# Weighted expert sums on TensorE: gate-diagonal matmuls into PSUM, LayerNorm statistics read from PSUM, and half-size loads

## The chip, the cores and the metric

The kernel runs on one core of one Trainium2 chip. Its engines are TensorE (PE, with its weight loads PEld), VectorE (DVE), ScalarE (ACT), GpSimd (POOL) and SyncE (SP), which here issues most DMA transfers. The metric is the device time of one execution in microseconds, as the median of three runs.

## The reference, cut to what matters

Two decoder layers; each ends in a mixture of experts whose two expert outputs per token are added, weighted by their gates, to the scaled residual, and normalized:

```
for layer in range(DEPTH):                      # 2 layers, 1024 tokens x 1024
    mix = gated_deltanet(...) or differential_attention(...)
    h = layer_norm(ALPHA * h + mix, ln_mix_g[layer], ln_mix_b[layer])
    ffn = hierarchical_moe(h, ...)              # y = sum over a token's 2 experts of gate * y_rows
    h = layer_norm(ALPHA * h + ffn, ln_ffn_g[layer], ln_ffn_b[layer])
```

All of it is float32. The change touches the last two lines, for both layers.

## The kernel before

Tokens stand in eight tiles of 128 rows (`NT = 8`). `experts` writes the expert outputs, unweighted, to a DRAM tensor, two rows per token (`y1` in the first layer, called layer 0 here, `y2` in layer 1). `combine` (L1785) then makes the sums and the normalization tile by tile. Its inner function `load` brings both expert rows of a tile (`yin`, 128 x 2 x 1024, 1 MB); the residual tile `c.h[t]` (a buffer named `mraw` in the profile) is already there for t < 5. `first` weights the first expert row on ACT (L1812) and makes two DVE steps out of the rest (L1815, L1816). `second` calls `normalize`, where DVE takes the statistics (L245, L247) and ACT computes 1/sigma in `rstd` (L232 to L237: a logarithm, an exponential and four small steps); what follows depends on `way`: 1 is DVE (L258), ACT (L260), POOL (L261); 2 is ACT and two POOL steps; 0 is two DVE steps (L258, L263). In layer 0 `second` also turns the tile with eight TensorE transposes into `hT`, the operand of the next projections, which the attention phase then uses; layer 1 writes the result.

An ACT function needs its table set to be active. The compiler puts a table load (ACT_TABLE_LOAD) ahead of an instruction whose function the active set lacks; for a logarithm or an exponential it may pick a set that lacks the other of the two. The kernel can also ask for a set by name. `first` does so at t == 0 (L1814): `natural_log_exp_and_others`, which holds both. Between that load in layer 0 and the next one no other set is asked for, so the attention phase, which comes next, runs with it: the softmax exponentials (L1114), and `norm`, which is called 32 times (8 heads, every second of 8 query tiles) and holds a square (L1140), a logarithm (L1143) and an exponential (L1144) on ACT, and a DVE step (L1145).

In the attention phase TensorE's instructions are interleaved: transposes of a softmax tile (`atr`, L1131), scores (L1100 to L1102), value products, and as filling the projections of the next heads (`pj`, L223 to L225), whose results ACT and DVE cast into two parts (`khh`/`kll`, `vT`). Each engine works its instructions off in the order that the scheduler has fixed; `tc.keep_in_program_order` and priorities bear on that order, and an instruction with no operands may move far in it.

Of the kernel before, what the change touches and what calls it, by code (L numbers as in the profile page):

```python
# [9 lines left out]
F32 = mybir.dt.float32  # L10
# [4 lines left out]
AF = mybir.ActivationFunctionType  # L15
OP = mybir.AluOpType
AX = mybir.AxisListType
PSUM = bass.MemoryType.PSUM

P = 128  # L20
D = 1024
T = 1024
KT = 8
NT = 8
# [3 lines left out]
ALPHA = 4.0 ** 0.25  # L28
# [23 lines left out]
CAH = 1  # L52

HA = ((2, 5), (2, 5))
YB = (3, 8)
LGT = 1
WAYS = ((1,) * 6 + (0,) * 2, (1,) * 6 + (0,) * 2, (1,) * 6 + (0,) * 2, (1, 2, 1, 2, 1, 2, 0, 0))
WB = 2
CAPS = (
    (96, 96, 80, 128, 128, 112, 112, 104, 96, 96, 88, 88, 80, 80, 80, 80) + (64,) * 8 + (56,) * 3 + (48,) * 5,  # L60
# [70 lines left out]
def instruction(i):  # L131
    return getattr(i, "ins", i)


def row_bc(ap, n):
    return bass.AP(tensor=ap.tensor, offset=ap.offset, ap=[[0, P], [1, n]])
# [91 lines left out]
def rstd(c, sd, mv):  # L228

    act = c.nc.scalar.activation  # L230
    r, v, w = (sd[:, i:i + 1] for i in range(3))
    act(w, mv[:, 1:2], AF.Ln, bias=c.ln_eps, scale=1.0)  # L232
    act(v, mv[:, 1:2], AF.Identity, bias=c.half_eps, scale=-0.5)
    act(r, w, AF.Exp, scale=-0.5)
    act(w, r, AF.Square)
    act(w, w, AF.Identity, bias=c.three_half, scale=v)  # L236
    act(r, r, AF.Copy, scale=w)  # L237


def normalize(c, lp, a, lg, lb, way):  # L240

    nc = c.nc
    st = lp.tile([P, 2, 6], F32, name="ln_st")
    for k in range(2):
        nc.vector.bn_stats(st[:, k, :], a[:, k * 512:(k + 1) * 512])  # L245
    mv = lp.tile([P, 2], F32, name="ln_mv")
    nc.vector.bn_aggr(mv, st)  # L247
    sd = lp.tile([P, 4], F32, name="ln_sd")
    rstd(c, sd, mv)
    r, m = sd[:, 0:1], sd[:, 3:4]  # L250
    if way == 2:
        nc.scalar.activation(m, mv[:, 0:1], AF.Copy, scale=-1.0)
        nc.scalar.activation(m, m, AF.Copy, scale=r)
        nc.scalar.activation(a, a, AF.Identity, scale=r, bias=m)
        nc.gpsimd.tensor_tensor(a, a, lg, OP.mult)
        nc.gpsimd.tensor_tensor(a, a, lb, OP.add)
        return
    nc.vector.scalar_tensor_tensor(a, a, mv[:, 0:1], lg, op0=OP.subtract, op1=OP.mult)  # L258
    if way == 1:
        nc.scalar.activation(a, a, AF.Copy, scale=r)  # L260
        nc.gpsimd.tensor_tensor(a, a, lb, OP.add)  # L261
    else:
        nc.vector.scalar_tensor_tensor(a, a, r, lb, op0=OP.mult, op1=OP.add)  # L263
# [573 lines left out]
def out_proj(c, res, part, layer, h_dram):  # L837
# [4 lines left out]
    with ExitStack() as es:  # L842
# [41 lines left out]
        def norm(n, t, a):  # L884
            normalize(c, lp, a, lg, lb, WAYS[layer][n])
            nc.sync.dma_start(h_dram[t * P:(t + 1) * P], a)
# [898 lines left out]
def combine(c, layer, h_dram, y_dram, dst, hT=None):  # L1785

    nc, tc, ins = c.nc, c.tc, c.ins
    with ExitStack() as es:
        yp = es.enter_context(tc.tile_pool(reuse_waits="tile", name="c_y", bufs=YB[layer]))
        lp = es.enter_context(tc.tile_pool(reuse_waits="tile", name="c_l", bufs=3))  # L1790
        ps = es.enter_context(tc.tile_pool(reuse_waits="tile", name="c_ps", bufs=2, space=PSUM))
        lg, lb = c.w.tile(), c.w.tile()
        c.h += [c.w.spare() for t in range(HA[layer][1], NT)]
        yv = y_dram.rearrange("(t p k) f -> t p k f", p=P, k=2)

        ys = []

        def load(t):

            ys.append(yp.tile([P, 2, D], F32, name="yin"))  # L1800
            with tc.issue_after(c.load0) if t else ExitStack():
                c.load0 = instruction(nc.sync.dma_start(ys[t], yv[t]))
                if t == LGT:
                    nc.sync.dma_start(lg, row_bc(ins["ln_ffn_g"][layer], D))
                    nc.sync.dma_start(lb, row_bc(ins["ln_ffn_b"][layer], D))
                if t >= HA[layer][1]:
                    nc.sync.dma_start(c.h[t], h_dram[t * P:(t + 1) * P])

        def first(t):
            n = TILES[layer].index(t)  # L1810
            y, a = ys[t], c.h[t]
            nc.scalar.activation(y[:, 0], y[:, 0], AF.Copy, scale=c.gates[:, n, 0:1])  # L1812
            if t == 0:
                tc.keep_in_program_order(nc.scalar.preload_act_table_set("natural_log_exp_and_others"))  # L1814
            nc.vector.scalar_tensor_tensor(a, a, ALPHA, y[:, 0], op0=OP.mult, op1=OP.add)  # L1815
            nc.vector.scalar_tensor_tensor(a, y[:, 1], c.gates[:, n, 1:2], a, op0=OP.mult, op1=OP.add)  # L1816
            return t, a

        def second(t, a):
            normalize(c, lp, a, lg, lb, WAYS[2 + layer][t])  # L1820
            store = nc.gpsimd if layer == 0 and WAYS[2][t] else nc.sync
            store.dma_start(dst[t * P:(t + 1) * P], a)
            if hT is not None:
                for gr in range(2):
                    pt = ps.tile([P, 4, P], F32, name="ctr")
                    for i in range(4):
                        k = gr * 4 + i
                        nc.tensor.transpose(pt[:, i], a[:, k * P:(k + 1) * P], c.ident)
                    sl = slice(t * P, (t + 1) * P)
                    kk = slice(gr * 4, gr * 4 + 4)  # L1830
                    nc.scalar.copy(hT[0][:, kk, sl], pt)
                    nc.vector.tensor_tensor(hT[1][:, kk, sl], pt, hT[0][:, kk, sl].bitcast(F32), OP.subtract)


        for t in range(NT):
            while len(ys) < min(NT, t + YB[layer]):
                load(len(ys))
            second(*first(t))
            if layer == 0 and t >= WB:
                c.bp.start(t - WB)  # L1840
    c.raw2.close()
# [25 lines left out]
def build(c, out):  # L1867
    nc, tc = c.nc, c.tc
    with ExitStack() as es:
# [11 lines left out]
        with ExitStack() as ws:  # L1881
            phase_a(c, ws, p1, h1)
            with ExitStack() as ms:
                experts_open(c, ms)
                routing(c, 0)
                c.first_b = [c.ins["w_kvq"][i] for i in (0, 16, 8)]
                experts(c, 0, h1, y1)
            bs = es.enter_context(ExitStack())
            hp = bs.enter_context(tc.tile_pool(reuse_waits="tile", name="hT", bufs=1))
            hT = [hp.tile([P, KT, T], F32R, tag=f"hT{i}", name=f"hT{i}") for i in range(2)]  # L1890
            ps = bs.enter_context(ExitStack())
            phase_b_open(c, ps)
            combine(c, 0, h1, y1, h2, hT)
        phase_b_attention(c, hT, hp, h2, p2)
        ps.close()
        with ExitStack() as ws:
            weights_open(c, 1, ws)
            out_proj(c, h2, p2, 1, h3)
            bs.close()
            with ExitStack() as ms:  # L1900
                experts_open(c, ms)
                routing(c, 1)
                experts(c, 1, h3, y2)
            combine(c, 1, h3, y2, out)
# [18 lines left out]
```

## Time and profile before

| what | value |
|---|---|
| time, median of 3 runs | 2758.09 us (2755.68 to 2760.45) |
| the profiled execution | 2756.32 us, span 2754.4 us |
| busy, of the span | PE 88%, DVE 55%, ACT 44%, POOL 20% |
| combine of layer 0 | about 1361 to 1434 us |
| attention phase | about 1434 to 1970 us |
| combine of layer 1, up to the end | about 2692 to 2754 us |

The span is the profiled part of the execution; 1.9 us lie around it. Shares over the whole span mix stages with different limits, so each of the three stages has to be read by itself.

### The profile page before, as it was taken

How to read it: one execution, taken by the hardware profiler on the slowest of the kernel's cores; microseconds unless marked ns; L12 is line 12 of the kernel's file. 1: busy time of each engine (PE TensorE's matmuls, PEld its weight loads, DVE VectorE, ACT ScalarE, POOL GpSimd, SP SyncE). 2: the span in 40 equal slices, each digit the busy share in tenths (PEclk: the TensorE clock that was granted, in tenths of full speed). 3: DMA queues.
4: the chain of work that ended last, by engine and by line, in shares of the span. 5: the costliest groups of instructions: out<-in, count | busy, mean ns of one | idle time of the engine just before them, and what ended most of it. 6: DMA issues, size and time to landing. Idle time of an engine off the chain costs nothing. (4 is left out here: it accounts for less than half of the span.)

```text
span 2754.4 us, 38782 instructions
## 1 busy us (share of the span) xinstructions
PE 2419.5 (88%) x13789; PEld 1647.4 (60%) x13789; DVE 1506.7 (55%) x2696; ACT 1213.4 (44%) x2173; POOL 550.5 (20%) x445
## 2 busy tenths in 40 slices
PE   8999999999979988889559999998987898999990
PEld 5777777776745544444248777776764464455560
DVE  4555555564547555555385676667436323333567
ACT  5455555543325544444255555555332212223454
POOL 3333333331212110110132111111011101111104
PEclk9999999999989999999769999999997999999995
DMA  4111111124779999999841111012536968899995
GB/s 146 49 58 51 55 59 47 58 76 130 252 257 351 392 386 381 384 380 397 339 157 45 31 33 39 32 32 82 165 145 245 399 232 341 304 352 361 361 362 226
DMA packets 195478, 564.00 MB, mean 205 GB/s; under 512 B 40400, under 2 KB 63184, under 8 KB 193232
## 3 DMA queue, kind: packets, MB, share of 16 engines
q1 hardware_dynamic: 178240, 515.07, 50.8%
q0 software_dynamic: 15168, 43.01, 4.5%
q10 hardware_dynamic: 1872, 3.40, 0.4%
q8 instruction: 110, 1.80, 0.3%
q14 instruction: 88, 0.72, 0.1%
HBM read 515.58 MB, written 52.89 MB: 206 GB/s over the span
## 5 line engine op out<-in xcount | busy, mean ns | idle before, releaser
L210 DVE TENSOR_TENSOR ml<-mraw,mh 128x1024 fp32r<-128x1024 f32 x300 | 357.1, 1221 | 248.0 <-ACT mh L210 228.2
L210 ACT CAST mh<-mraw 128x1024 fp32r<-128x1024 f32 x300 | 306.5, 1052 | 247.5 <-DMA mraw<-in_w 196.0
L210 PE MATMUL acc<-mh,xT 128*128 128x512 f32 (+5 forms) x976 | 328.5, 405 | 1.6 <-ACT mh L210 1.6
L210 PE MATMUL acc<-mraw,xTw 128*64 128x512 f32 x1184 | 288.8, 620 | 16.4 <-DVE xTw L210 16.3
L185 POOL TENSOR_TENSOR wl<-raw,wh 128x512 fp32r<-128x512 f32 x106 | 155.1, 1484 | 484.7 <-ACT wh L184 420.5
L210 PEld LDWEIGHTS acc<-mh,xT 128*128 128x128 f32 (+5 forms) x976 | 166.5, 171 | 87.9 <-issue 18.6
L223 PE MATMUL pj<-xh,wh 128*128 128x512 f32 x512 | 217.6, 425 | 0.0
L224 PE MATMUL pj<-xl,wh 128*128 128x512 f32 x512 | 209.2, 409 | 0.0
L225 PE MATMUL pj<-xh,wl 128*128 128x512 f32 x512 | 207.5, 405 | 0.1
L1581 POOL DMA_INDIRECT X<-h,xidx x69 | 71.5, 1037 | 679.2 <-PE mtw L210 354.5
L210 PE MATMUL acc<-ml,xT 128*128 128x512 f32 (+5 forms) x496 | 195.9, 399 | 0.8 <-DVE ml L210 0.8
L223 PE MATMUL pj<-hT,wh 128*128 128x512 f32 (+1 forms) x432 | 166.0, 384 | 8.9 <-DVE kll L1010 5.4
L224 PE MATMUL pj<-hT,wh 128*128 128x512 f32 (+1 forms) x432 | 167.9, 389 | 0.0
L210 PEld LDWEIGHTS acc<-mraw,xTw 128*64 128x64 f32 x1184 | 76.9, 139 | 151.7 <-issue 109.7
L225 PE MATMUL pj<-hT,wl 128*128 128x512 f32 (+1 forms) x432 | 162.4, 376 | 1.6 <-POOL wl L185 1.6
L210 PE MATMUL acc<-mh,hT 128*128 128x512 f32 (+5 forms) x480 | 159.1, 402 | 0.2
L210 PE MATMUL acc<-mraw,hTw 128*64 128x512 f32 x592 | 140.5, 618 | 14.1 <-ACT hTw L210 14.0
L408 DVE SCALAR_TENSOR_TENSOR cv<-pr,cw,cv 128x512 f32<-128x512 f32 x144 | 118.9, 826 | 50.7 <-ACT cv L405 48.7
L1114 ACT ACTIVATE e<-sc,sm 128x256 f32<-128x256 f32 (+7 forms) x128 | 94.5, 741 | 89.8 <-DVE sm L1112 89.4
L210 PEld LDWEIGHTS acc<-mh,hT 128*128 128x128 f32 (+5 forms) x480 | 82.6, 172 | 49.6 <-issue 14.6
L225 PEld LDWEIGHTS pj<-xh,wl 128*128 128x128 f32 x512 | 96.9, 189 | 19.9 <-POOL wl L185 0.6
L224 PEld LDWEIGHTS pj<-xl,wh 128*128 128x128 f32 x512 | 97.3, 190 | 17.9 <-issue 1.4
(407 smaller groups left out, 4923.9 us busy)
## 6 DMA issues: line engine op xcount, KB each, us to landing
mraw<-in_w SPq DMA_DIRECT2D x720, 512.0 KB, 10.7
raw<-in_w_in SPq DMA_DIRECT2D x32, 512.0 KB, 3.5
yin<-y SPq DMA_DIRECT2D x16, 1024.0 KB, 7.0
raw<-in_w_kvq SPq DMA_DIRECT2D x21, 512.0 KB, 3.5
h<-res SPq DMA_DIRECT2D x16, 512.0 KB, 3.2
p<-ores POOLq DMA_DIRECT2D x12, 512.0 KB, 4.3
res<-p SPq DMA_DIRECT2D x12, 512.0 KB, 5.5
mh<-in_w SPq DMA_DIRECT2D x12, 512.0 KB, 6.8
```

Source lines behind the costliest of these rows:

```text
L185: c.nc.gpsimd.tensor_tensor(l[:, s], src[:, s], h[:, s].bitcast(F32), OP.subtract)
L210: out = getattr(self.engine, name)(*args, **kwargs)
L223: mm(out, ah, bh, start=first, stop=False)
L224: mm(out, ah, bl, start=False, stop=False)
L225: mm(out, al, bh, start=False, stop=last)
L408: nc.vector.scalar_tensor_tensor(a, pr[:, 1 + j:513 + j], cw[:, idx, j:j + 1], a, op0=OP.mult, op1=OP.add)
L1114: nc.scalar.activation(e[:, 0:L], st[m][:, 0:L], AF.Exp, bias=sm[:, 2 + m:3 + m], scale=SC, accum_out=sm[:, 4 + m:5 + m])
L1581: c.last_gather = instruction(nc.gpsimd.indirect_dma_start(out=b.X[0:rows], out_offset=None, in_=h_dram, in_offset=bass.IndirectOffsetOnAx ...
```

## The change

`combine` makes the weighted sum on TensorE. Three DVE instructions build `diag`: 17 matrices of 128 x 128, sixteen with the gates of one tile and one expert slot on the diagonal, one with ALPHA. A tile's sum is then, for each half of 512 columns, a float32 matmul of `diag` with each of the two expert rows, and, where the new table `RESP` says 1, one with the residual (2 tiles in layer 0, 6 in layer 1; the other eight add the residual by one DVE step on PSUM). `SUMS` gives the number of PSUM buffers. `normalize` reads statistics and its first pass from that sum in PSUM. The expert rows are loaded in halves of 512 KB, `YB` counts halves, and layer 1 uses way 1 where it used way 2 in turn. The request for the table set stands ahead of the loops.

```diff
-YB = (3, 8)
+YB = (4, 16)
-WAYS = (..., (1, 2, 1, 2, 1, 2, 0, 0))
+WAYS = (..., (1,) * 6 + (0,) * 2)
+RESP = ((1, 1, 0, 0, 0, 0, 0, 0), (1, 1, 1, 1, 1, 0, 1, 0))
+SUMS = (2, 4)
...
-        nc.vector.bn_stats(st[:, k, :], a[:, k * 512:(k + 1) * 512])
+        nc.vector.bn_stats(st[:, k, :], src[:, k * 512:(k + 1) * 512])
...
-    nc.vector.scalar_tensor_tensor(a, a, mv[:, 0:1], lg, op0=OP.subtract, op1=OP.mult)
+    nc.vector.scalar_tensor_tensor(a, src, mv[:, 0:1], lg, op0=OP.subtract, op1=OP.mult)
...
+        diag = dp.tile([P, 2 * NT + 1, P], F32, name="diag")
+        nc.vector.tensor_scalar(diag[:, 2 * NT], c.ident, ALPHA, None, op0=OP.mult)
+        gates = c.gates.rearrange("p t k -> p (t k)")
+        for q in (slice(0, 4), slice(4, 2 * NT)):
+            n = q.stop - q.start
+            nc.vector.tensor_tensor(diag[:, q], c.ident[:, None, :].to_broadcast([P, n, P]),
+                                    gates[:, q, None].to_broadcast([P, n, P]), OP.mult)
...
-            ys.append(yp.tile([P, 2, D], F32, name="yin"))
+            ys.append([yp.tile([P, D], F32, name="yin") for k in range(2)])
...
-                c.load0 = instruction(nc.sync.dma_start(ys[t], yv[t]))
+                for k in range(2):
+                    c.load0 = instruction(nc.sync.dma_start(ys[t][k], yv[t][:, k]))
...
+        def add(t, w, src, start, stop):
+            for f in range(2):
+                h = slice(f * 512, (f + 1) * 512)
+                nc.tensor.matmul(sums[t][:, h], diag[:, w], src[:, h], start=start, stop=stop)
+
+        def residual(t):
+            if t < NT:
+                sums[t] = ps.tile([P, D], F32, name="sum")
+                if RESP[layer][t]:
+                    add(t, 2 * NT, c.h[t], True, False)
...
         def first(t):
             n = TILES[layer].index(t)
-            y, a = ys[t], c.h[t]
-            nc.scalar.activation(y[:, 0], y[:, 0], AF.Copy, scale=c.gates[:, n, 0:1])
-            if t == 0:
-                tc.keep_in_program_order(nc.scalar.preload_act_table_set("natural_log_exp_and_others"))
-            nc.vector.scalar_tensor_tensor(a, a, ALPHA, y[:, 0], op0=OP.mult, op1=OP.add)
-            nc.vector.scalar_tensor_tensor(a, y[:, 1], c.gates[:, n, 1:2], a, op0=OP.mult, op1=OP.add)
+            for k in range(2):
+                add(t, 2 * n + k, ys[t][k], k == 0 and not RESP[layer][t], k == 1)
+            if not RESP[layer][t]:
+                nc.vector.scalar_tensor_tensor(sums[t], c.h[t], ALPHA, sums[t], op0=OP.mult, op1=OP.add)
...
+        tc.keep_in_program_order(nc.scalar.preload_act_table_set("natural_log_exp_and_others"))
+        for t in range(SUMS[layer]):
+            residual(t)
         for t in range(NT):
-            while len(ys) < min(NT, t + YB[layer]):
+            while len(ys) < min(NT, t + YB[layer] // 2):
                 load(len(ys))
-            second(*first(t))
+            first(t)
+            second(t)
+            residual(t + SUMS[layer])
```

What the scheduler makes of it on ACT in the combine of layer 0, from the last instruction ahead of it (`lm`, of the attention's setup). Before:

```order
L981 ACT_TABLE_LOAD
L981 ACTIVATE lm<-lm 128x2
L1812 ACTIVATE yin<-yin,gates 128x1024
L1814 ACT_TABLE_LOAD
L1812 ACTIVATE yin<-yin,gates 128x1024
L232 ACTIVATE ln_sd<-ln_mv,ct_all 128x1
L233 ACTIVATE ln_sd<-ln_mv,ct_all 128x1
L234 ACTIVATE ln_sd<-ln_sd 128x1
L235 ACTIVATE ln_sd<-ln_sd 128x1
L236 ACTIVATE ln_sd<-ln_sd,ct_all 128x1
L237 ACTIVATE ln_sd<-ln_sd 128x1
```

And in the changed kernel (lines are three or four higher: L235 is the logarithm, L237 the exponential):

```order
L985 ACT_TABLE_LOAD
L985 ACTIVATE lm<-lm 128x2
L235 ACT_TABLE_LOAD
L235 ACTIVATE ln_sd<-ln_mv,ct_all 128x1
L236 ACTIVATE ln_sd<-ln_mv,ct_all 128x1
L237 ACT_TABLE_LOAD
L237 ACTIVATE ln_sd<-ln_sd 128x1
L238 ACTIVATE ln_sd<-ln_sd 128x1
L239 ACTIVATE ln_sd<-ln_sd,ct_all 128x1
L240 ACTIVATE ln_sd<-ln_sd 128x1
L264 ACTIVATE mraw<-mraw,ln_sd 128x1024
```

The request for the joint set (now L1860) has moved out of this place: it stands at the head of layer 0's `experts`, and again at the head of layer 1's, each time just ahead of the load that the experts' SiLU needs. From there on a logarithm and the exponential behind it each have a load of their own, in all sixteen tiles of the two combines.

ACT at one of the 32 calls of `norm` in the attention phase. Before:

```order
L1114 ACTIVATE e,sm<-sc,sm 128x896 x2
L1140 ACTIVATE sq<-po 128x256
L1143 ACTIVATE sq<-pr,ct_all 128x256
L1144 ACTIVATE sq<-sq 128x256
L1084 COPY vT<-pj 128x512
L1035 CAST vh<-vtr 128x512
```

In the changed kernel:

```order
L1118 ACTIVATE e,sm<-sc,sm 128x896 x2
L1144 ACTIVATE sq<-po 128x256
L1147 ACT_TABLE_LOAD
L1147 ACTIVATE sq<-pr,ct_all 128x256
L1148 ACT_TABLE_LOAD
L1148 ACTIVATE sq<-sq 128x256
L1088 COPY vT<-pj 128x512
L1039 CAST vh<-vtr 128x512
```

The order of the other instructions is the same; all 32 calls have these two loads (64 in all; one of them falls to the softmax exponential behind the logarithm). Over the whole program ACT's list holds 168 table loads where it held 72.

TensorE in the combine of layer 0. Before, `ctr` being the transposes and `pj` the first projection:

```order
L1758 UNCONDITIONAL_BRANCH
L1828 MATMUL ctr<-ct_all,mraw 128x128 x16
L223 MATMUL pj<-hT_12017,wh 128x256
L224 MATMUL pj<-hT_12018,wh 128x256
L225 MATMUL pj<-hT_12017,wl 128x256
```

In the changed kernel, `sum` being the new sums:

```order
L1828 MATMUL sum<-mraw,diag 128x512 x4
L1828 MATMUL sum<-yin,diag 128x512 x11
L1854 MATMUL ctr<-ct_all,mraw 128x128 x8
L1828 MATMUL sum<-yin,diag 128x512 x4
L1854 MATMUL ctr<-ct_all,mraw 128x128 x8
L1828 MATMUL sum<-yin,diag 128x512
L226 MATMUL pj<-hT_12017,wh 128x256
```

The last matmul of tile 2's sum now stands behind the transposes of tile 0, and that of tile 3 behind the transposes of tile 1; the sums of tiles 4 to 7 stand behind the first projection pieces, in the same manner.

## Rows read from the trace of the kernel before

**Rows 1.** By stage: length, then busy PE, PEld, DVE, ACT, POOL; clock; DMA.
```profile
1361.00:1434.00 73.00, 27.65 (x122) 23.81 (x123) 68.00 (x75) 41.91 (x92) 30.66 (x19) 0.55 0.62 231
1434.00:1970.00 536.00, 508.50 (x2783) 418.97 (x2782) 360.62 (x776) 295.93 (x658) 77.48 (x50) 0.99 0.14 44
2692.00:2754.40 62.40, 0.00 (x0) 0.00 (x0) 50.32 (x47) 29.29 (x69) 26.97 (x9) 0.50 0.61 244
```

**Rows 2.** What TensorE waited for, 1434 to 1970: total us, times, longest.
```profile
PE atr L1131 <- DVE e L1124: 16.3, 22, 1.5
```

**Rows 3.** Timeline of TensorE (start, us): a float32 matmul; a restart after idling.
```profile
231.90 1.02 PE L699 MATMUL pr<-sq,ct_all 128*128 128x512 f32 x2
232.76 0.38 PE L680 MATMUL sc<-qd,S 128*128 128x128 f32 x2
...
1429.86 0.58 PE L223 MATMUL pj<-hT,wh 128*128 128x256 f32 x1 [3.75 <-DVE kll L1010]
...
1434.93 0.31 PE L225 MATMUL pj<-hT,wl 128*128 128x256 f32 x1
```

**Rows 4.** Timeline of ACT around a table load in phase A.
```profile
161.66 0.28 ACT L685 ACTIVATE sq<-sc 128x128 f32<-128x128 f32 x1 [0.44 <-PE sc L681]
161.96 1.28 ACT L702 ACT_TABLE_LOAD   x1
163.25 0.63 ACT L702 ACTIVATE sq<-sq 128x512 f32<-128x512 f32 x1
```

**Rows 5.** Timeline of one head's four norms in the attention phase.
```profile
1600.69 0.47 ACT L1143 ACTIVATE sq<-pr,ct_all 128x256 f32<-128x256 f32 x1 [0.33 <-PE pr L1142]
...
1604.29 0.48 ACT L1134 CAST ah<-atr 128x384 fp32r<-128x384 f32 x1 [0.70 <-PE atr L1131]
...
1611.29 0.66 PE L1131 MATMUL atr<-ct_all,e 128*128 128x128 f32 x4 [0.46 <-DVE e L1124]
...
1616.84 0.47 ACT L1143 ACTIVATE sq<-pr,ct_all 128x256 f32<-128x256 f32 x1
...
1618.28 0.87 DVE L1124 SCALAR_TENSOR_TENSOR e<-e,sm 128x640 f32<-128x640 f32 x1
...
1619.31 0.73 PE L1131 MATMUL atr<-ct_all,e 128*128 128x128 f32 x5
...
1637.32 0.47 ACT L1143 ACTIVATE sq<-pr,ct_all 128x256 f32<-128x256 f32 x1 [0.79 <-PE pr L1142]
...
1638.49 0.59 ACT L1084 COPY vT<-pj 128x512 f32<-128x512 f32 x1 [0.24 <-PE pj L225]
...
1639.22 0.60 PE L1033 MATMUL vtr<-ct_all,vT 128*128 128x128 f32 x4
...
1655.73 0.47 ACT L1143 ACTIVATE sq<-pr,ct_all 128x256 f32<-128x256 f32 x1
...
1656.44 0.27 PE L1131 MATMUL atr<-ct_all,e 128*128 128x128 f32 x1
```

**Rows 6.** Timeline of POOL's last step and TensorE's transposes, layer 0.
```profile
1398.84 3.20 POOL L261 TENSOR_TENSOR mraw<-mraw 128x1024 f32<-128x1024 f32 x1 [2.41 <-ACT mraw L260]
...
1402.09 1.97 PE L1828 MATMUL ctr<-ct_all,mraw 128*128 128x128 f32 x8 [3.56 <-POOL mraw L261]
```

**Rows 7.** Timeline of the combine of layer 1, up to the last DVE instruction.
```profile
2693.05 0.80 SPq L1802 DMA_DIRECT2D yin<-y  x2
...
2704.15 0.29 ACT L232 ACTIVATE ln_sd<-ln_mv,ct_all 128x1 f32<-128x1 f32 x1 [2.63 <-DVE ln_mv L247]
...
2705.41 0.29 ACT L237 ACTIVATE ln_sd<-ln_sd 128x1 f32<-128x1 f32 x1
...
2706.61 1.15 ACT L260 ACTIVATE mraw<-mraw,ln_sd 128x1024 f32<-128x1024 f32 x1 [0.91 <-DVE mraw L258]
...
2712.62 1.29 DVE L245 BATCH_NORM_STATS2 ln_st<-mraw 128x6 f32<-128x512 f32 x2
...
2749.47 1.28 DVE L263 SCALAR_TENSOR_TENSOR mraw<-mraw,ln_sd 128x1024 f32<-128x1024 f32 x1 [0.31 <-ACT ln_sd L237]
```

More of the change, by code (lines that the diff above doesn't have):

```diff
@@ L54 @@
 HA = ((2, 5), (2, 5))
-YB = (3, 8)
+YB = (4, 16)
 LGT = 1
-WAYS = ((1,) * 6 + (0,) * 2, (1,) * 6 + (0,) * 2, (1,) * 6 + (0,) * 2, (1, 2, 1, 2, 1, 2, 0, 0))
+WAYS = ((1,) * 6 + (0,) * 2, (1,) * 6 + (0,) * 2, (1,) * 6 + (0,) * 2, (1,) * 6 + (0,) * 2)
+RESP = ((1, 1, 0, 0, 0, 0, 0, 0), (1, 1, 1, 1, 1, 0, 1, 0))
+SUMS = (2, 4)
 WB = 2
@@ L237, in rstd, with normalize @@
     act(r, r, AF.Copy, scale=w)
-def normalize(c, lp, a, lg, lb, way):
+def normalize(c, lp, a, lg, lb, way, src=None):
     nc = c.nc
+    src = a if src is None else src
     st = lp.tile([P, 2, 6], F32, name="ln_st")
     for k in range(2):
-        nc.vector.bn_stats(st[:, k, :], a[:, k * 512:(k + 1) * 512])
+        nc.vector.bn_stats(st[:, k, :], src[:, k * 512:(k + 1) * 512])
     mv = lp.tile([P, 2], F32, name="ln_mv")
@@ L253, in normalize @@
         nc.scalar.activation(m, m, AF.Copy, scale=r)
-        nc.scalar.activation(a, a, AF.Identity, scale=r, bias=m)
+        nc.scalar.activation(a, src, AF.Identity, scale=r, bias=m)
         nc.gpsimd.tensor_tensor(a, a, lg, OP.mult)
@@ L1790, in combine @@
         lp = es.enter_context(tc.tile_pool(reuse_waits="tile", name="c_l", bufs=3))
-        ps = es.enter_context(tc.tile_pool(reuse_waits="tile", name="c_ps", bufs=2, space=PSUM))
+        dp = es.enter_context(tc.tile_pool(reuse_waits="tile", name="c_d", bufs=1))
+        ps = es.enter_context(tc.tile_pool(reuse_waits="tile", name="c_ps", bufs=SUMS[layer], space=PSUM))
         lg, lb = c.w.tile(), c.w.tile()
+        diag = dp.tile([P, 2 * NT + 1, P], F32, name="diag")
[5 more added lines that the diff above has]
+                                    gates[:, q, None].to_broadcast([P, n, P]), OP.mult)
         c.h += [c.w.spare() for t in range(HA[layer][1], NT)]
@@ L1807, in load, with second @@
                     nc.sync.dma_start(c.h[t], h_dram[t * P:(t + 1) * P])
+        sums = {}
+        def add(t, w, src, start, stop):
[7 more added lines that the diff above has]
+                    add(t, 2 * NT, c.h[t], True, False)
         def first(t):
             n = TILES[layer].index(t)
-            y, a = ys[t], c.h[t]
-            nc.scalar.activation(y[:, 0], y[:, 0], AF.Copy, scale=c.gates[:, n, 0:1])
-            if t == 0:
-                tc.keep_in_program_order(nc.scalar.preload_act_table_set("natural_log_exp_and_others"))
-            nc.vector.scalar_tensor_tensor(a, a, ALPHA, y[:, 0], op0=OP.mult, op1=OP.add)
-            nc.vector.scalar_tensor_tensor(a, y[:, 1], c.gates[:, n, 1:2], a, op0=OP.mult, op1=OP.add)
-            return t, a
-        def second(t, a):
-            normalize(c, lp, a, lg, lb, WAYS[2 + layer][t])
+            for k in range(2):
+                add(t, 2 * n + k, ys[t][k], k == 0 and not RESP[layer][t], k == 1)
+            if not RESP[layer][t]:
+                nc.vector.scalar_tensor_tensor(sums[t], c.h[t], ALPHA, sums[t], op0=OP.mult, op1=OP.add)
+        def second(t):
+            a = c.h[t]
+            normalize(c, lp, a, lg, lb, WAYS[2 + layer][t], sums[t])
             store = nc.gpsimd if layer == 0 and WAYS[2][t] else nc.sync
@@ L1824, in second @@
                 for gr in range(2):
-                    pt = ps.tile([P, 4, P], F32, name="ctr")
+                    pt = c.bp.ps.tile([P, 4, P], F32, tag="tr", name="ctr")
                     for i in range(4):
```

## The prediction, made before the changed kernel was run

> **What bounds the kernel now.** I first read the table of stages. The combine of layer 0 (1361 to 1434) keeps DVE busy for 68.0 of 73 us, that of layer 1 (2692 to the end) for 50.3 of 62.4 with TensorE at rest, and the attention phase between them keeps TensorE busy for 508.5 of 536 us, ACT for 295.9 [rows 1]. So DVE sets the two combines and TensorE the attention phase. Next I read what TensorE waits for in that phase: mostly the softmax mix ahead of the transposes, 22 times and 16.3 us in all, 0.7 us each [rows 2]. That chain is tight: at 22 places there is no slack at all, and a delay of ACT or DVE goes through to TensorE.
>
> **What is removed.** One ACT pass for each of the sixteen tiles, and two DVE passes for each, of which eight tiles keep one on PSUM. DVE loses 24 passes of 1.28 us (the length of the last one in the trace [rows 7]), some 30 us over both stages, more where POOL slowed it. That is the gain if nothing else ends later.
>
> **What is added on TensorE.** A float32 matmul of 512 columns takes 232.76 - 231.90 = 0.86 us at full clock (2.4 GHz) [rows 3], twice that at the lower level (1.2 GHz). Layer 0 gets (8 x 2 + 2) x 2 = 36, layer 1 (8 x 2 + 6) x 2 = 44, that is 31 and 38 us at full clock. After a wait of 3.75 us TensorE ran at the lower level from 1429.86 to 1434.93, 5.1 us, before it rose [rows 3].
>
> **What is added on ACT, which only the program's list shows.** The request for the joint table set is hoisted to the head of `experts`, where the SiLU's load overwrites it. So there is a load for each logarithm and one for the exponential behind it: 16 in each combine, 64 in the attention phase. One in phase A takes 1.28 us; it starts 0.02 us after the instruction ahead has ended, and the exponential starts 0.01 us after it [rows 4]. So the price is 1.28 us each, with nothing around it. A load has no operand to wait for: the first of a pair can fill a gap that ACT has anyway; the second can't.
>
> The Trainium skill ("ScalarE: Activation LUTs", What ACT_TABLE_LOAD costs) gives the same 1283 ns but adds a drain of about 1380 ns, 2.66 us for each switch; by it the pairs would take about 170 us of ACT in the attention phase (an estimate from that page) where the row gives 82. Rows 4 show no such drain, and I go by them.
>
> **Attention, +54 us.** There are 32 norms; I follow the four of one head, which differ [rows 5].
> - At 1600.69 ACT had idled 0.33 us before the logarithm, so the exponential is 2.57 - 0.33 = 2.24 late, and the casts behind it too, until the cast of the transposes at 1604.29, before which ACT idled 0.70: 1.5 us are left. Score maxima, exponentials and the mix follow, and the transposes at 1611.29 wait already (0.46). Cost 1.5.
> - At 1616.84 ACT had no gap. DVE's step of the norm waits for the exponential, and the mix at 1618.28 stands behind it on DVE. It ended at 1619.15, the transposes began at 1619.31: 2.57 - 0.16 = 2.4.
> - At 1637.32 there is a gap of 0.79, and 0.24 before the copy at 1638.49, which the transposes at 1639.22 need: 1.5. TensorE works in order, so all behind them is late.
> - At 1655.73 there is no gap. The transposes at 1656.44 start 0.24 us after the logarithm ended; I take it that they need its PSUM buffer. One load stands before that: 1.3.
>
> Together 6.7 us a head, 54 for eight. The bounds: 19 if only the second kind reaches TensorE, 82 if all 64 loads do.
>
> **Layer 0's combine, +8 us.** DVE loses 10 passes (16 go, 6 come back), 12.8 us of its 68.0. ACT's 41.9 us lose eight passes of 1.15 [rows 7] and gain 16 loads: 53 of 73. Only two sums fit in PSUM, and the last matmul of tile t + 2 stands behind the transposes of tile t on TensorE, which wait for POOL, which waits for ACT. A round of two tiles is then: transposes 2.0 and POOL 3.2 [rows 6], the matmul, a DVE pass and statistics (2.8), `rstd` with its loads (4.1, below) and scale (1.15), about 15 us; the other tile's ACT work, 6.3 us with its two casts (0.48 for 384 columns [rows 5], more for 512), falls in between in part, so I take 17. Four rounds are 68; the first tile comes some 5 us later since TensorE starts cold, and the projection pieces ahead of the sums of tiles 4 and 6 add some 8 (48 matmuls of 256 columns at about 0.2 us, partly beside other work): 81 us in place of 73. Bounds: -8 (DVE still the limit, most of its 12.8 gone) and +20 (all 16 loads on the path).
>
> **Layer 1's combine, -2 us.** TensorE begins with 8 residual matmuls near 2693 [rows 7]: three in the cold 5.1 us, five at 0.86, then four for tile 0 by 2705.9, its statistics (1.29 [rows 7], 1.5 with the aggregation) by 2707.4; ACT began at 2704.15 before. From here DVE needs about 2.8 us a tile and TensorE 3.4 to 5.2, but ACT needs `rstd` 1.55 (2704.15 to 2705.41 + 0.29), two loads 2.57 and the scale 1.15 [rows 7]: 5.27 us for each of six tiles, 4.12 for the other two. ACT becomes the limit. Its first load is over before the statistics are: 2707.4 + 3.99 + 5 x 5.27 + 4.12 = 2741.9 for the seventh tile's `rstd`. Behind that stand, in DVE's order, its last pass (1.28), the last tile's statistics (1.5), its `rstd` (2.83, one load hidden) and last pass (1.28): 2748.8, against 2749.47 + 1.28 = 2750.8 [rows 7], which is -2.0. Bounds: -10 if TensorE is warm and ACT's loads are hidden in part; +14 if TensorE stays at the lower level (44 x 1.72 = 76 us from 2693, so its last sum at 2769, less what its waits for the rows would give back). The half-size loads bring the same bytes in the same order; only tile 0 could gain a fraction of a microsecond, which the cold TensorE hides. `diag` costs DVE three passes over 2176 columns in all, two microseconds or three, in layer 0 before the rows land, in layer 1 among the last experts.
>
> **Sum.** 54 + 8 - 2 = +60 on 2756.3, the profiled execution, 1.8 us under the median of the runs: 2816 on that scale, 2818 as a median. I say 2816.
>
> **Rivals.**
> - *The loads hide in attention* (faster). ACT has 240 us idle there and 82 are added [rows 1]. If the filling projections cover the delays, attention costs nothing and the combines decide: with DVE as their limit they give back 8 and 10 us, 2738. It decides where each norm's delay stays under the slack of the chain; rows 2 and the second norm of rows 5 show none. Chance 0.04; with a dearer combine, within 0.2% of 2758 (5.5 us, about what a measurement tells from no change), another 0.04.
> - *The loads do not come between logarithm and exponential.* ACT would need 2.7 us a tile in layer 1, and both combines would end early: 2738 too. Against it: phase A has such a load right ahead of an exponential [rows 4]. Chance 0.02. The Trainium skill ("ScalarE: Activation LUTs", Table sets: the hidden batching unit) says that a logarithm and the exponential behind it need one load, since one set has both; the trace disagrees here, as its rows show the second load.
> - *Each switch costs double.* A stall as long as the load, behind each one, would lift 54 to about 137 (64 x 1.3 more) and the combines by up to 30: 2900 to 2930. The gaps of rows 4 speak against it. Chance 0.03. The drain quoted above would do this.
> - *TensorE at its lower clock becomes the limit of both combines*: +14 and +20 on top of attention, 2844. For it: the granted clock was 0.55 and 0.50 in these stages [rows 1]. Against it: the new matmuls stand close together. Chance 0.12.
>
> **How the numbers follow.** The forecast with its bounds has 0.75. Attention is its widest term: between 25 and 75 us of it, with -3 to +14 for the combines, give 2778 to 2846, and that also holds half of the clock case, 8 in 10 together. Slower by over 0.2% has 0.90, no change 0.04, faster 0.06.
>
> **What would show it.** Table loads of 1.28 us at 64 places in attention; each head longer by some 6.7 us; TensorE waiting longer on the mix; in layer 1's combine ACT, not DVE, without gaps, and DVE near 2.8 us a tile. The forecast is wrong if the attention phase stays at 536 us, or if TensorE's clock in layer 1's combine stays at 0.50.

## The result, and the profile after

The changed kernel took 2804.15 us (median of four runs, 2802.54 to 2806.23) where the kernel before took 2758.11 beside it: a ratio of 1.017, 95% interval 1.0154 to 1.0186. The prediction said 2816, between 2778 and 2846. The profiled execution is the one of 2802.54 us, span 2800.4; against the span of before, 2754.4, that is +46.0.

The stages after, in the columns of [rows 1] (length; busy time of PE, PEld, DVE, ACT, POOL; clock; DMA). The attention phase now reaches to 2020:

```profile
1361.00:1434.00 73.00, 52.38 (x209) 31.20 (x208) 43.96 (x66) 53.67 (x100) 25.06 (x18) 0.90 0.66 241
1434.00:2020.00 586.00, 521.99 (x2765) 422.44 (x2765) 357.43 (x773) 376.56 (x719) 75.66 (x50) 0.98 0.13 41
2738.00:2800.40 62.40, 40.47 (x88) 17.57 (x88) 27.07 (x36) 39.96 (x70) 14.05 (x6) 0.83 0.62 244
```

DVE is down from 68.0 to 44.0 us in the combine of layer 0 and from 50.3 to 27.1 in that of layer 1, and TensorE runs there at a granted clock of 0.90 and 0.83 in place of 0.55 and 0.50. Yet neither stage is much shorter, since ACT has 12 and 11 us more; and the attention phase is 50 us longer. I measure the stages by marks that every kernel here has: a combine from the first load of expert rows on SP's queue to the last hT step on DVE (layer 0) or the end of the span (layer 1), the attention phase from the first norm's logarithm to the last one's.

| between the marks, us | before | after | |
|---|---|---|---|
| combine of layer 0 | 77.6 | 75.1 | -2.5 |
| attention, first to last norm | 492.7 | 543.4 | +50.7 |
| last norm to first load of layer 1's combine | 724.8 | 719.8 | -5.0 |
| combine of layer 1 | 61.4 | 62.0 | +0.6 |

Starts are read to a tenth of a us, so differences of these can be off by 0.1. The rest, +2.2, is a start of layer 0's combine that is 1.65 later and 0.6 between it and the first norm. What made the -5.0 is open: in the twelve kernels below that stretch took between 722 and 730 us, in one execution each, with or without the loads, a spread wider than the 5.0.

The groups of table loads on ACT by line, in the whole span (count; busy us, mean ns; idle time before them):

```profile
L1147 ACT ACT_TABLE_LOAD x32 | 41.1, 1283 | 0.6
L1148 ACT ACT_TABLE_LOAD x31 | 39.8, 1283 | 0.6
...
L235 ACT ACT_TABLE_LOAD x16 | 20.5, 1283 | 4.8 <-issue 4.5
L237 ACT ACT_TABLE_LOAD x16 | 20.5, 1283 | 0.3
...
L1118 ACT ACT_TABLE_LOAD x1 | 1.3, 1283 | 0.0
```

The 64 of the attention phase and the 32 of the combines are all there, each 1.283 us. What TensorE waited for from 1434 to 2030, against [rows 2] (total us, times, longest):

```profile
PE atr L1135 <- DVE e L1128: 32.9, 24, 2.4
PE vtr L1037 <- ACT vT L1088: 9.5, 8, 1.5
PE atr L1135 <- ACT sq L1147: 8.4, 9, 1.3
```

The wait on the mix has doubled (16.3 before). The two others are the third and the fourth norm of the prediction's head: the copy `vT` 1.2 us late on average, once for each head, a wait that TensorE did not have before; the logarithm 0.9 on average, nine times, where it was waited for once before (0.8 us).

The start of layer 1's combine on ACT, which answers to [rows 7]:

```profile
2738.57 1.28 ACT L235 ACT_TABLE_LOAD   x1 [4.51 <-issue]
2753.72 0.29 ACT L235 ACTIVATE ln_sd<-ln_mv,ct_all 128x1 f32<-128x1 f32 x1 [13.87 <-DVE ln_mv L251]
...
2754.22 1.28 ACT L237 ACT_TABLE_LOAD   x1
2755.52 0.20 ACT L237 ACTIVATE ln_sd<-ln_sd 128x1 f32<-128x1 f32 x1
...
2756.74 1.15 ACT L264 ACTIVATE mraw<-mraw,ln_sd 128x1024 f32<-128x1024 f32 x1
2757.90 1.28 ACT L235 ACT_TABLE_LOAD   x1
...
2763.37 1.28 ACT L235 ACT_TABLE_LOAD   x1
```

The first load is over long before the statistics, as predicted. From then on ACT has no gap for seven tiles and takes 5.47 us a tile (2757.90 to 2763.37), while DVE waits for it, 8.65 us in one place:

```profile
2752.15 1.30 DVE L249 BATCH_NORM_STATS2 ln_st<-sum 128x6 f32<-128x512 f32 x2 [17.36 <-PE sum L1828]
...
2789.56 1.28 DVE L267 SCALAR_TENSOR_TENSOR mraw<-mraw,ln_sd 128x1024 f32<-128x1024 f32 x1 [8.65 <-ACT ln_sd L240]
```

### The profile page after: what moved, and what is told of

Same layout as the page of the kernel before. It is cut to its first block, busy times and chain, and to the rows that moved or that the text cites. A ratio compares the mean times of both kernels' runs of the same rounds, so it can differ in the third digit from the quotient of the medians.

```text
span 2800.4 us, 39191 instructions
## 1 busy us (share of the span) xinstructions
PE 2502.9 (89%) x13949; PEld 1679.2 (60%) x13949; DVE 1462.0 (52%) x2681; ACT 1320.9 (47%) x2247; POOL 532.8 (19%) x442
## 4 chain that ended last, share of the span: by engine, by line
PE 46%; DMA 21%; DVE 14%; ACT 11%; issue 4%; POOL 2%; SPq 0%; ACTq 0%; another core or an unknown queue 0%; DVEq 0%; POOLq 0%
DMA mraw<-in_w 18%; PE acc L213 18%; PE pj L227 4%; PE pj L226 4%; PE pj L228 4%; PE po L227 2%; PE po L226 2%; PE po L228 2%; DVE tmp L558 2%; DVE cv L412 1%; ACT L1147 1%; DVE sm L1115 1%; PE atr L1135 1%; ACT e L1118 1%; DVE ml L213 1%
## 5 line engine op out<-in xcount | busy, mean ns | idle before, releaser
L213 PE MATMUL acc<-mraw,hTw 128*64 128x512 f32 x592 | 147.7, 644 | 22.8 <-ACT hTw L213 22.7
L412 DVE SCALAR_TENSOR_TENSOR cv<-pr,cw,cv 128x512 f32<-128x512 f32 x144 | 119.0, 827 | 50.9 <-ACT cv L409 48.9
L213 PEld LDWEIGHTS acc<-mraw,hTw 128*64 128x64 f32 x592 | 43.4, 147 | 112.3 <-issue 74.6
```

The costliest lines, as they stand in the source:

```text
L213: out = getattr(self.engine, name)(*args, **kwargs)
L412: nc.vector.scalar_tensor_tensor(a, pr[:, 1 + j:513 + j], cw[:, idx, j:j + 1], a, op0=OP.mult, op1=OP.add)
```

## The experiments

My theory: the loads, which came in because the request lost its place, cost all of the lengthening, and the sums on TensorE by themselves gain. The main rival: the sums, their clock, the PSUM operands or the smaller transfers cost something of their own. The first four kernels take the two apart.

**e1_pinned: the change with the request held in its place.**

```diff
         def first(t):
             n = TILES[layer].index(t)
+            if t == 0:
+                nc.scalar.copy(lp.tile([P, 1], F32, name="pin", bufs=1), ys[0][0][:, 0:1])
+                tc.keep_in_program_order(nc.scalar.preload_act_table_set("natural_log_exp_and_others"))
...
-        tc.keep_in_program_order(nc.scalar.preload_act_table_set("natural_log_exp_and_others"))
         for t in range(SUMS[layer]):
```

> The changed kernel with one thing put back: the request for the joint table set stands behind a one-column copy of the first expert row on ACT, so that it stays at the head of each combine and its set holds through the attention phase; ACT's list has 72 loads in place of 168. Theory (the loads are the cost): the attention phase gives back its 50.6 us, ACT needs about 2.9 us a tile in place of 5.5 in layer 1's combine, which ends about 8 us sooner, that of layer 0 some 5 us; the 4 us that the experts of layer 1 gained are lost again: 2804 - 51 - 8 - 5 + 4 = 2744 us, under the kernel before. Rival 1 (the loads are only beside the cost, which comes from the sums on TensorE, the statistics from PSUM or the half-size loads): 2804, unchanged. Rival 2 (the loads cost in the attention phase alone, the combines hide them): about 2757, level with the kernel before.

2739.4 us (2735.67 to 2742.06), ratio to before 0.993 (0.9917 to 0.9944): faster than before. Its norms, with the first and the last start, and its two combines:

```profile
L1147 ACT ACTIVATE sq<-pr,ct_all x32: 465/474/477, 1464.0 to 1958.4; 128x256 f32<-128x256 f32 x32
```

```profile
1358.00:1423.00 65.00, 52.25 (x211) 30.78 (x211) 46.11 (x73) 34.91 (x88) 25.13 (x18) 0.92 0.77 279
...
2683.60:2735.30 51.70, 40.38 (x88) 17.57 (x88) 26.96 (x36) 20.06 (x56) 14.11 (x6) 0.90 0.75 294
```

The theory had 2744. Attention is back at 494.4 us, and ACT has 20.1 us in place of 40.0 in layer 1's combine, which is 10.3 shorter; layer 0's is 11.0 shorter, where the theory had 8 and 5. One more line of the change, `pt = c.bp.ps.tile([P, 4, P], F32, tag="tr", name="ctr")`, is in every figure for the sums and is taken apart by no run: the transposes' result takes its PSUM buffers from the attention phase's pool and no longer from `combine`'s own, where the sums now are.

**e2_before_moved: the kernel before, with only the request moved.**

```diff
-            if t == 0:
-                tc.keep_in_program_order(nc.scalar.preload_act_table_set("natural_log_exp_and_others"))
...
+        tc.keep_in_program_order(nc.scalar.preload_act_table_set("natural_log_exp_and_others"))
         for t in range(NT):
```

> The kernel before with only the request moved ahead of the loops, as the change has it; sums, statistics and loads as before. Theory: the same 64 loads in the attention phase cost about 50 us there, the 16 in each combine up to 10 us each, since DVE, not ACT, sets those stages: 2806 to 2825, 2815 us. Rival (the loads cost nothing by themselves): 2758.

2823.65 us (2821.34 to 2827.34), ratio 1.0238 (1.022 to 1.0256). Its norms, with their loads:

```profile
L1143 ACT ACT_TABLE_LOAD  x32: 1283/1283/1283, 1483.1 to 2026.6; - x32
L1143 ACT ACTIVATE sq<-pr,ct_all x32: 474/474/477, 1484.4 to 2027.9; 128x256 f32<-128x256 f32 x32
```

Without any of the new sums the attention phase takes 543.5 us, as in the changed kernel. The combines lose 10.2 and 6.0 us; the theory had 2815 in all.

**e3_attn_pinned and e4_attn_loads: the loads in one half only.** The first holds the request at the head of the attention phase, the second (on e1_pinned) asks there for the exponential's own set:

```diff
-    nc.scalar.preload_act_table_set("natural_log_exp_and_others")
+    tc.keep_in_program_order(nc.scalar.preload_act_table_set("natural_log_exp_and_others"))
...
+    tc.keep_in_program_order(nc.scalar.preload_act_table_set("exp_and_others"))
```

> The changed kernel with the request at the head of the attention phase held in its place, behind the combine of layer 0: the 64 loads of the attention phase go, the 32 of the combines stay. Theory: 2804 - 51 + 4 = 2757 us, and the stage lengths of both combines as in the changed kernel (about 72 and 62 us). Rival (the attention phase became longer by what the combine leaves behind, not by its loads): 2804.

> The other half: the first of these kernels (request held in both combines) with a request for the exponential's own set at the head of the attention phase, so that the 64 loads come there and none in the combines. Theory: 50 us longer than the first of these kernels less the 4 us in layer 1's experts, about 2790 us, and its attention phase as long as in the changed kernel (543 us between the first and the last norm). Rival: as the first of these kernels.

2757.51 us (ratio 0.9998, 0.9986 to 1.0009) and 2789.96 us (1.0117, 1.01 to 1.0133). The six kernels side by side, in us between the marks:

| sums | loads | combine 0 | attention | combine 1 | median |
|---|---|---|---|---|---|
| DVE, ACT (before) | none | 77.6 | 492.7 | 61.4 | 2758 |
| DVE, ACT (e2) | both | 87.8 | 543.5 | 67.4 | 2824 |
| TensorE (e1) | none | 64.1 | 494.4 | 51.7 | 2739 |
| TensorE (e3) | combines | 75.2 | 493.8 | 62.3 | 2758 |
| TensorE (e4) | attention | 65.6 | 543.3 | 51.6 | 2790 |
| TensorE (after) | both | 75.1 | 543.4 | 62.0 | 2804 |

Each stage depends on its own loads alone. The sums give 13.5 and 9.7 us in the combines; the loads take 11 and 10.3 of that back, and cost 49 to 51 in attention. The main rival is out.

These are one profiled execution each, and a stage repeats itself only so well. In e1, e4 and the later e5, e9, e10 and e12 TensorE, DVE and POOL do the same instructions in the same order in layer 0's combine, without loads, and it took 64.1, 65.6, 63.2, 66.8, 65.1 and 67.8 us. So the sums give some 10 to 14 us there, and between two of these kernels a difference of under 4 us in that stage is not shown. Layer 1's combine is steadier: 51.4 to 52.2 us in e1, e4, e9, e10 and e12.

**e7_copied and e8_warm_before: where the 13.5 come from.** The first puts the sums back into SBUF ahead of the statistics, the second gives the kernel before matmuls whose result nobody reads:

```diff
+            nc.scalar.copy(a, sums[t])
-            normalize(c, lp, a, lg, lb, WAYS[2 + layer][t], sums[t])
+            normalize(c, lp, a, lg, lb, WAYS[2 + layer][t])
...
+            if layer == 0:
+                for f in (0, 512, 0, 512):
+                    nc.tensor.matmul(warm, c.ident, y[:, 1, f:f + 512], start=True, stop=True)
```

> On the kernel with the request held (2739 us): ACT copies each finished sum from PSUM into the tile in SBUF, and the statistics and the first pass read that copy, so that they are as before the change while the sums stay on TensorE. Adds 16 copies of about 1.15 us on ACT. Theory (reading PSUM is what freed DVE and POOL of each other: a pass took up to 3.4 us beside POOL before and 1.28 after, a POOL step 3.2 and 2.34): DVE passes from SBUF stretch to 2 us and more beside POOL again and POOL's steps to 3 us; combine of layer 0 about 70 in place of 64.2, layer 1 about 54 in place of 51.7: 2748. Rival (fewer passes alone freed them): passes stay at 1.28, only the copies' delay shows, 1 to 2 us a stage: 2742.

> The kernel before, with four float32 matmuls for each tile of layer 0's combine that read the expert row and write a PSUM tile which nobody reads; nothing else changes (DVE and ACT still make the sums). It asks what the higher granted clock gives by itself. Theory (DVE sets that stage, busy 68 of 73 us): transposes go from 1.97 to about 1.1 us, but the stage gets at most 2 to 3 us shorter than its 77.7: 2755 to 2758. Rival (the clock is most of the 13.5 us that the sums on TensorE gain there): 2747 to 2750. Rival (the matmuls delay the transposes): up to 2765.

e7_copied took 2744.29 us (ratio 0.9947, 0.9927 to 0.9966; e1_pinned 0.993). DVE's first pass and POOL's addition in layer 0's combine (count; busy us, mean ns; idle), of e1_pinned:

```profile
L262 DVE SCALAR_TENSOR_TENSOR mraw<-sum,ln_mv,mraw 128x1024 f32<-128x1024 f32 x8 | 10.2, 1279 | 1.4 <-DMA mraw<-in_ln_ffn_g 1.2
...
L265 POOL TENSOR_TENSOR mraw<-mraw 128x1024 f32<-128x1024 f32 x6 | 14.1, 2351 | 22.1 <-ACT mraw L264 22.1
```

and of e7_copied:

```profile
L262 DVE SCALAR_TENSOR_TENSOR mraw<-mraw,ln_mv 128x1024 f32<-128x1024 f32 x8 | 16.5, 2063 | 0.4
...
L265 POOL TENSOR_TENSOR mraw<-mraw 128x1024 f32<-128x1024 f32 x6 | 15.9, 2658 | 24.0 <-ACT mraw L264 23.9
```

The same pass takes 1.28 us with one operand in PSUM and 2.06 on average with both in SBUF (2.12 before the change). The averages hide two cases. Here is one pass beside one of POOL's additions in e7_copied, and then in e1_pinned:

```profile
1376.90 2.34 POOL L265 TENSOR_TENSOR mraw<-mraw 128x1024 f32<-128x1024 f32 x1 [16.04 <-ACT mraw L264]
1377.12 3.20 DVE L262 SCALAR_TENSOR_TENSOR mraw<-mraw,ln_mv 128x1024 f32<-128x1024 f32 x1
```

```profile
1372.10 2.36 POOL L265 TENSOR_TENSOR mraw<-mraw 128x1024 f32<-128x1024 f32 x1 [14.45 <-ACT mraw L264]
1372.24 1.28 DVE L262 SCALAR_TENSOR_TENSOR mraw<-sum,ln_mv,mraw 128x1024 f32<-128x1024 f32 x1
```

In e7_copied the two passes of that stage that met no work of POOL's took 1.28 us as well. The Trainium skill ("SBUF — State Buffer", SBUF: two separate sides) says that a DVE operation with two SBUF inputs and a GpSimd operation that reads SBUF exclude each other; the trace agrees, 3.20 against 1.28. So the theory holds for the passes. Its prices for the stages do not: layer 0's combine took 66.0 us where it had 70, which is within the scatter around e1_pinned, and layer 1's 57.4 where it had 54; the copies on ACT are in both, and the run doesn't tell what the passes cost by themselves.

e8_warm_before took 2755.18 us (ratio 0.9988, 0.9977 to 1.0). The granted clock of its combine is 0.80, that of before 0.54, and the stage is 74.4 us in place of 77.7, with DVE still at 66:

```profile
1358.00:1434.00 76.00, 52.67 (x197) 31.88 (x198) 66.42 (x79) 42.11 (x94) 30.02 (x19) 0.80 0.65 239
```

The clock, as far as it rose here, gives 3.3 us of the 13.5 by the stage and 2.1 by the time, both hardly more than the noise; the rival that had it as most of the gain (2747 to 2750) is out. I put what is left down to DVE's passes that are gone; no run takes these away by themselves.

**e6_whole_loads: transfers of 1 MB again.**

```diff
-                for k in range(2):
-                    c.load0 = instruction(nc.sync.dma_start(ys[t][k], yv[t][:, k]))
+                c.load0 = instruction(nc.sync.dma_start(y, yv[t]))
```

> On the kernel with the request held (2739 us): expert rows come by one transfer of 1 MB for each tile again, as before the change, in as many buffers. Theory (as predicted: same bytes in the same order): within 1 us in both combines, 2739 to 2740. Rival (halves let the first sum start earlier): combine of layer 0 longer by 2 to 3 us, that of layer 1, where the residual matmuls cover the landing, unchanged: 2742.

2737.86 us (ratio 0.9926, 0.9907 to 0.9945), not to be told from e1_pinned. Layer 0's combine took 67.2 us, from a first load that went out 3 us sooner to the same end, 1422.4. That is the 2 to 3 us more that the rival had and not the 1 of the theory; but it lies within the stage's scatter, and the instructions of the stage stand in another order too, so neither is shown there. Layer 1's took 51.5, as both had it.

**e9_first_only, e10_second_only, e12_both_planned: one load or the other.** Requests of their own in the norm of e1_pinned; the third kernel has both:

```diff
+            tc.keep_in_program_order(nc.scalar.preload_act_table_set("natural_log_exp_and_others"))
             nc.scalar.activation(sq, pr, AF.Ln, bias=c.rms_eps, scale=1.0 / P)
+            tc.keep_in_program_order(nc.scalar.preload_act_table_set("natural_log_exp_and_others"))
             nc.scalar.activation(sq, sq, AF.Exp, scale=-0.5)
```

> The kernel with the request held (2739 us, attention 494.4 us from the first norm's logarithm to the last) with one table load put in ahead of each of the 32 norms' logarithms, none between logarithm and exponential. By the gaps that the prediction counts, such a load costs 1.28 less 0.33 and 0.70 at the first norm of a head (0.25), 1.12 at the second, 0.25 at the third, 1.28 at the fourth: 2.9 us a head, 23 us for eight, 2762. Rival (each load costs alike, half of the 50.7 that both cost): 25, 2765. Rival (ACT's wait for the matmul of the squares hides it wholly): under 5, 2740 to 2744.

> The same with the 32 loads between logarithm and exponential, where ACT has no wait to fill. By the prediction's gaps: 0.58 at the first norm of a head (1.28 less 0.70), 1.12 at the second, 1.04 at the third (1.28 less 0.24), none at the fourth, where the transposes wait for the logarithm alone: 2.7 us a head, 22 us, 2761; with the 23 of the other half that is less than the 50.7 of both, since a gap filled by one load is not there for the second. Rival (each load costs alike): 25, 2765. Rival (only the second load costs): 45 to 50, 2785 to 2790.

2755.52 us (ratio 0.999, 0.9979 to 1.0001) and 2753.34 (0.9965, 0.9942 to 0.9987). Their norms:

```profile
L1148 ACT ACTIVATE sq<-pr,ct_all x32: 468/477/480, 1466.3 to 1974.9; 128x256 f32<-128x256 f32 x32
```

```profile
L1147 ACT ACTIVATE sq<-pr,ct_all x32: 468/477/478, 1465.9 to 1969.5; 128x256 f32<-128x256 f32 x32
```

Attention takes 508.6 and 503.6 us, +14.2 and +9.2, against the 23 and 22 that I worked out, and together far less than the 49 of e4_attn_loads. But these requests stand in the program when its order is set. By the traces TensorE, ACT and DVE go through the attention phase in another order than in e1_pinned, while in the changed kernel they keep that of e1_pinned, the loads apart. Hence the last run.

> The kernel with the request held (2739 us, attention 494.4 us between first and last norm) with both loads put in as requests of their own, one ahead of each logarithm and one ahead of each exponential: the same 64 loads at the same places as in the changed kernel. There the loads were put into a list whose order was set without them (TensorE's, DVE's and POOL's orders are those of the kernel with the request held, instruction for instruction); here, as with the two halves, the requests are there when the order is set, and projections and transposes change places around the norms. Theory 1 (the order, made with the loads in it, puts other work of TensorE where the norms are late): the halves add up, 14.2 + 9.2 = 23 us, attention 518 us, 2763. Theory 2 (a delay is free up to the slack of the chain, about a microsecond, and each one beyond it counts, whatever the order): as in the changed kernel, attention 543 us, 2788.

2768.32 us (ratio 1.0044, 1.0028 to 1.006), and attention 525.5:

```profile
L1148 ACT ACTIVATE sq<-pr,ct_all x32: 473/474/476, 1464.8 to 1990.3; 128x256 f32<-128x256 f32 x32
```

That is +31.1, between the two theories: 18 of the 49 us go when the order is made with the loads in it, and 31 remain, 8 more than the halves add up to. Two loads that share one slack would have it so; but the orders of the three kernels differ among themselves as well, so that is not shown.

**e5_res2 and e11_dve_only: from here to a faster kernel.** In e1_pinned TensorE has no gap in layer 1's combine, and its first 9.48 us go to residuals while DVE waits:

```profile
2684.27 9.48 PE L1828 MATMUL sum<-mraw,diag 128*128 128x512 f32 x16 [5.68 <-issue]
2693.58 7.03 PE L1828 MATMUL sum<-yin,diag 128*128 128x512 f32 x16
```

```diff
-RESP = ((1, 1, 0, 0, 0, 0, 0, 0), (1, 1, 1, 1, 1, 0, 1, 0))
+RESP = ((1, 1, 0, 0, 0, 0, 0, 0), (1, 1, 0, 0, 0, 0, 0, 0))
```

e11_dve_only also sets the third entry of `WAYS` to `(0,) * 8`. That gives DVE the last step of all eight tiles of layer 0; the entry chooses the queue of the stores too, so all eight tiles are stored from SP's queue where six had gone from POOL's.

> On the kernel with the request held (2739 us): in layer 1 only the first two tiles keep their residual on TensorE, the other six get it as a DVE pass on PSUM, as layer 0 has it. There TensorE had no gap from 2684.3 to 2724.6 while DVE waited 17 us for the first sum. Theory (TensorE is the limit of that combine now): 8 matmuls of 0.86 us go, 4 of them ahead of the first sum at the lower clock, and DVE, with 4.05 us for such a tile, ends about 5 us sooner: combine 51.7 to about 46, 2734 us. Rival (the rows from DRAM are the limit, their loads moving 294 GB/s over the stage): no change, 2739. Rival (DVE becomes the limit at once, four more passes of 1.23): up to +3, 2742.

> On the fastest kernel so far (request held, two residuals on TensorE in layer 1, 2732 us): in layer 0's combine DVE makes the last step of all eight tiles by itself (one pass of 1.28 us, as it does for the last two), in place of ACT's scale (1.15) and POOL's addition (2.35) for six. Theory (that stage is set by the way from statistics to transposes, TensorE waits 5 times for POOL and DVE is idle for a third of it): a tile's way is 2.2 us shorter, DVE has 50 of some 60 us, and the stage ends 4 to 6 us sooner: 2727. Rival (DVE becomes the limit there): 0 to +3, 2732 to 2735.

e5_res2: 2731.99 us (ratio 0.9902, 0.9885 to 0.9919), layer 1's combine 46.9. Its first two rows on TensorE:

```profile
2687.68 5.98 PE L1828 MATMUL sum<-mraw,diag 128*128 128x512 f32 x8 [5.59 <-issue]
2693.50 27.63 PE L1828 MATMUL sum<-yin,diag 128*128 128x512 f32 x64
```

e11_dve_only: 2730.47 us (0.9896, 0.9879 to 0.9913), not to be told from it. The theory had 4 to 6 us off layer 0's combine, and it was wrong: the stage took 66.2 us where that of e5_res2 took 63.2, with DVE at 52.7 of them and the clock at 0.86 in place of 0.93. The 3.0 are within the stage's scatter, so that it became longer is not shown, and neither is why nothing was gained.

## Why the prediction was right, by its steps

**Attention, +54: the loads are the cause, the size 50.7.** e2, e3 and e4 give 50.8, 49.6 and 48.9 for the same 64 loads. The first six heads took 7.0 us more each (their 24 norms 417.8 us for 375.5) where the prediction had 6.7. The second head before, and the second and third after, in the columns of [rows 1]:

```profile
1538.12:1600.69 62.57, 59.97 (x321) 49.01 (x320) 43.46 (x95) 35.90 (x81) 9.69 (x6) 1.00 0.11 34
```

```profile
1545.13:1614.93 69.80, 61.17 (x322) 48.70 (x321) 43.63 (x94) 46.09 (x89) 9.71 (x6) 1.00 0.10 31
1614.93:1684.35 69.42, 62.31 (x322) 50.15 (x321) 42.84 (x94) 46.28 (x89) 9.19 (x6) 0.98 0.10 31
```

What TensorE waited for in the second head, before and after:

```profile
PE atr L1131 <- DVE e L1124: 2.4, 3, 1.5
```

```profile
PE atr L1135 <- DVE e L1128: 5.6, 4, 2.4
PE vtr L1037 <- ACT vT L1088: 1.2, 1, 1.2
PE atr L1135 <- ACT sq L1147: 1.1, 1, 1.1
PE pj L226 <- DVE kll L1014: 0.5, 1, 0.5
```

So the waits are those that the prediction named, and each is somewhat shorter: 3.2 us more on the mix for its 1.5 and 2.4, 1.2 for the copy's 1.5, 1.1 for the logarithm's 1.3, together 5.5 for 6.7. A wait on `kll` (0.5) that it did not name, and 1.2 us more of busy time on TensorE, for which no run here shows a reason, bring the head to 7.2. That the total fits so well is in part luck. In four of the first six heads the mean granted clock was 0.98 and in two 1.00; the four took 69.4 to 69.9 us and the two 69.8, so the clock is not what lengthened them.

The prediction was too high for the last two heads: from 1851.01 to 1968.21 before and 1892.99 to 2018.56 after, they cost 8.4 together and not 13.4; why they are cheaper I did not test. That the gaps in single rows also give the price of one load alone is not borne out (14.2 and 9.2 for 23 and 22); since the order changed with those requests, it stays open for an unchanged one.

**Layer 0's combine, +8: the term of the projection pieces was wrong.** It came out at -2.5. TensorE's transposes (`ctr`) of tiles 0, 2, 4 and 6 in the changed kernel, and the first and the last piece (`pj`) of the block between the first two:

```profile
1375.04 1.09 PE L1854 MATMUL ctr<-ct_all,mraw 128*128 128x128 f32 x8 [0.54 <-POOL mraw L265]
...
1381.91 0.68 PE L226 MATMUL pj<-hT,wh 128*128 128x256 f32 x1
...
1388.38 0.28 PE L226 MATMUL pj<-hT,wh 128*128 128x256 f32 x1
...
1392.76 1.04 PE L1854 MATMUL ctr<-ct_all,mraw 128*128 128x128 f32 x8
...
1407.99 1.09 PE L1854 MATMUL ctr<-ct_all,mraw 128*128 128x128 f32 x8 [3.29 <-POOL mraw L265]
...
1424.59 1.06 PE L1854 MATMUL ctr<-ct_all,mraw 128*128 128x128 f32 x8 [2.80 <-DVE ln_mv L251]
```

Rounds of 17.7, 15.2 and 16.6 us, where 17 was said: that was right. But the pieces lie within these rounds, as the block from 1381.91 to 1388.66 does, and I added 8 for them on top; without that the sum is 73 us from 1361, and the last step ended at 1433.7.

**Layer 1's combine, -2: right in kind, +0.6 in size.** ACT is without gaps at 5.47 us a tile for 5.27 (six tiles: 1.2 us), and its first logarithm stood 15.3 us behind the first load of rows for the 14.4 predicted, since TensorE's residual matmuls began 0.7 us after that load (2739.11) and not with it. The residual matmuls themselves took 9.57 us, for the 9.4 in the sum.

**The sum.** +46.0 on the profiled execution for +60: attention 3.3 less, layer 0 10.5 less, layer 1 2.6 more, the 5.0 of layer 1's experts less, 2.2 more at and behind the start of layer 0's combine. The last two had no term in the prediction.

**The rivals.** The loads don't hide in attention (e3 against the changed kernel: 49.6 us), they do come between logarithm and exponential (the rows at L237), a load has 0.01 to 0.02 us around it and no stall of its own length, and TensorE's clock in the combines rose to 0.90 and 0.83 with the new matmuls, so its lower level did not become their limit.

## What to carry to other kernels

An instruction without operands has only the place that something holds it at: when the one ahead of it goes, look in the program's list where it went, and count the loads on ACT. Here that one line turned a gain of 0.7% into a loss of 1.7%. A saving and a slip in one change add up stage by stage, so measure a stage between marks that both kernels have, and put one part of the change alone into each kernel. One profiled execution tells a stage no better than the stage repeats itself: here 63.2 to 67.8 us in one and 51.4 to 52.2 in another, for the same instructions.

## What was not expected of the hardware

An operand in PSUM did more than it was predicted to: the pass of DVE went from 2.06 to 1.28 us on average (3.20 to 1.28 beside one of POOL's additions) and POOL's addition from 2.66 to 2.35 when the sum was read from PSUM (e7_copied, e1_pinned); statistics from PSUM cost the same as from SBUF, 0.685 and 0.683 us. And the price of a load is one of the order around it: the same 64 loads, between the same instructions of ACT, cost 49 us of attention in one order and 31 in another.
